# Layer 0's last output projection: channel blocks 4-7 first in its first chunk, weights in half tiles, added rows in two pools

## The chip, the cores and the metric

The kernel runs on one core of a Trainium2 chip. The metric is the device time of one execution in microseconds, given as the median of several runs. One execution was recorded by the hardware profiler; its rows are counted from the start of its span.

## The reference, cut to what matters

The reference is one inference step of a two-layer decoder trunk (a hybrid layer 0, a sparse-attention layer 1) over 1024 prompt tokens and 8 sample tokens; the kernel treats them as one row of T = 1032 columns. Layer 0 has two branches, an SSD branch that gives y_a and a convolution branch that gives y_b, and ends with one output projection over both and a layer norm of the residual sum:

```
y = y.reshape(b, l, SSD_INNER) * silu(z_a)
y = y.reshape(b, l, SSD_GROUPS, SSD_INNER // SSD_GROUPS)
y = y * rsqrt(mean(square(y), -1, keepdims=True) + EPS)
y_a = y.reshape(b, l, SSD_INNER) * norm_g
...
out = concatenate([y_a, y_b], axis=-1) @ w_out
x_new = layer_norm(ALPHA * x + out, ln_g, ln_b)
```

The mean is taken per group: SSD_GROUPS is 2, so y_a's 1024 channels are two groups of 512. All arithmetic is in float32.

## The kernel before, in words

**Layout.** Channels lie on the 128 partitions, so 1024 channels are 8 blocks of [128, 1032]. Tokens are handled in three chunks of 344 columns (CH, line 22). A matrix product in full precision is three products: each operand is split into a high part in float32r and a low part that is the rest (hi by a ScalarE cast, lo by a subtraction on VectorE or GpSimd), and `mm3` (lines 125 to 135) adds w_hi x a_hi, w_hi x a_lo and w_lo x a_hi over the 8 channel blocks kt: 24 products for one output block m of one chunk. They stand on lines 132, 133 and 134 whoever calls `mm3`.

**Weights.** `load_half` (lines 101 to 110) loads half of a weight tile (512 columns, 4 channel blocks of one output block) into the staging ring `wst` of the pool `wpool` (3 buffers), casts it (L108) to `whi` and subtracts (L109) to `wlo`, 3 buffers each. All projections go through this ring, layer 1's too.

**The end of layer 0.** The output projection is cut in two. `out_b(m)` (lines 728 to 738) multiplies y_b's 8 blocks, held as 16 tiles `act` of the pool R1, with the weights OB + m, adds ALPHA times x (L737, VectorE) and stores the rows to the DRAM tensor `dpart` (L738). This is done while the SSD heads still run. Between the calls stands `gate(g, t0, n)` (lines 701 to 718), the gated norm of one group of one chunk: it loads four blocks of silu(z_a) from DRAM (L707), multiplies (L708, VectorE), squares (L709, ScalarE), adds the squares (L711, VectorE), takes the mean over the partitions with a product by a constant matrix (L714, TensorE), takes Ln and Exp (L174 and L175, ScalarE, each with a table load), and scales the four blocks (L718, VectorE). Blocks 4 to 7 (group 1) are finished first: out_b(1) to out_b(3) are followed by gate(1, ...) of the three chunks, out_b(4) to out_b(6) by gate(0, ...).

Then `halves` (lines 754 to 767) splits y_a into tiles `ya`: blocks 4 to 7 in whole rows, blocks 0 to 3 chunk by chunk (L756 casts on ScalarE; L757 subtracts, odd blocks on GpSimd, even ones on VectorE; the tiles show as yh, yl and yb). The eight weight tiles OA + m come whole, 1024 columns or 512 KB, through a pool `wst0` with 2 buffers (L775), and are cast (L776) and subtracted (L777, odd m on GpSimd) into the 16 `act` tiles of R1, which y_b leaves free after out_b(7). They stay there for the three chunks.

For each chunk the rows of `dpart` are loaded in two transfers of four blocks (L786, pool `parts0`, 4 buffers), each output block m gets its 24 products (L790) in a PSUM tile, `pp` (2 buffers) for even m and `pt` (5 buffers) for odd m, VectorE adds it to the rows (L791), and `layer_norm` (lines 800 to 833) follows; it writes x1 as new halves into `ya` and the rows to `dx1` by a DMA of GpSimd's queue (L793). Layer 1 begins with products of x1 (L158 for its indexer keys, L938 to L940 for its values).

**What sets the order.** Each engine runs its instructions in the order of its own queue, and every DMA here but L793 is issued by SyncE (SP), also in order. The order is not that of the program text: the program is built with a planner (`TileContext(nc, schedule_with_timeline_sim=True)`, line 1766) that walks through a simulated time and, on each engine, takes what is ready, what is earlier in the text first. Tiles of a pool are handed on from user to user, and a later pool takes the place of a closed one; who takes a place waits for the last user of it. `tc.issue_after(ins)` puts the instructions of a block that are on the engine of `ins` behind `ins`.

## Time and profile before

| | us |
|---|---|
| runs: median of 3 (lowest to highest) | 1704.07 (1701.54 to 1705.91) |
| the profiled execution | 1705.27 |
| its span, by which the rows count | 1703.5 |
| mean granted clock of TensorE in it | 0.973 of full speed |

The end of the OB products and the OA products lie at about 794 to 918 us of the span. In the rows, an engine is PE (TensorE; PEld is its weight load), DVE (VectorE), ACT (ScalarE), POOL (GpSimd) or SPq (SyncE issuing DMAs); L714 is line 714 of the kernel; `out<-in` are tiles by the program's names. Products overlap in TensorE's pipeline, so a product's own length is longer than the time between two starts.

### The profile page before, as it was taken

The page shows a single profiled execution, that of the slowest core. Times are in us where ns is not written, and L with a number is a line of the kernel's source. Part 1 is how long each engine was busy: PE and PEld are TensorE (multiplying, and loading weights), DVE is VectorE, ACT ScalarE, POOL GpSimd, SP SyncE. Part 2 cuts the span into 40 slices and gives each one's busy share as a digit, 9 for nine tenths or more (in the row PEclk, how much of TensorE's full clock was granted, in tenths as well). Part 3 has the DMA queues.
Part 4 walks back from the last instruction along what each step waited for, and adds up shares of the span by engine and source line. Part 5 has one row for each costly group of instructions (what it writes and reads, how often), then busy time and mean ns, then how long its engine had stood idle before and what let it go on. Part 6 is the DMA issues. An engine that isn't in the chain of part 4 may idle for free. (4 is left out here: it accounts for less than half of the span.)

```text
span 1703.5 us, 28787 instructions
## 1 busy us (share of the span) xinstructions
PE 1598.4 (94%) x10334; PEld 1437.5 (84%) x10334; DVE 1175.5 (69%) x2480; ACT 869.4 (51%) x1950; POOL 333.9 (20%) x670
## 2 busy tenths in 40 slices
PE   8999989989999998997998999888898899999996
PEld 7999989989999987996998999878897567676774
DVE  4788987460558787756565458999957866565663
ACT  5245523552445564535334445577774755545663
POOL 4000000001122243122422200144361410112120
PEclk9999999999999999998999999999999999999998
DMA  7332243453111254433421214422346424543460
GB/s 237 105 116 66 62 112 100 133 207 117 45 38 58 70 191 157 128 114 123 151 69 54 87 46 133 128 94 88 119 148 194 113 47 114 128 109 88 99 144 28
DMA packets 165650, 185.74 MB, mean 109 GB/s; under 512 B 20324, under 2 KB 131260, under 8 KB 165252
## 3 DMA queue, kind: packets, MB, share of 16 engines
q1 hardware_dynamic: 162996, 178.15, 35.4%
q0 software_dynamic: 1216, 4.37, 0.7%
q8 instruction: 81, 1.33, 0.3%
q10 hardware_dynamic: 1296, 1.38, 0.3%
q14 instruction: 61, 0.50, 0.1%
HBM read 131.91 MB, written 54.05 MB: 109 GB/s over the span
## 5 line engine op out<-in xcount | busy, mean ns | idle before, releaser
L132 PE MATMUL pp<-act,whi 128*128 128x344 f32 x1016 | 330.2, 327 | 12.5 <-ACT act L233 8.1
L134 PE MATMUL pp<-act,wlo 128*128 128x344 f32 x1016 | 331.1, 328 | 11.0 <-DVE wlo L109 11.0
L133 PE MATMUL pp<-act,whi 128*128 128x344 f32 x1016 | 330.4, 325 | 1.0 <-POOL act L726 0.8
L132 PEld LDWEIGHTS pp<-act,whi 128*128 128x128 f32 x1016 | 194.1, 192 | 15.8 <-ACT act L233 8.1
L134 PEld LDWEIGHTS pp<-act,wlo 128*128 128x128 f32 x1016 | 194.3, 192 | 13.3 <-DVE wlo L109 11.9
L133 PEld LDWEIGHTS pp<-act,whi 128*128 128x128 f32 x1016 | 194.3, 191 | 3.5 <-POOL act L726 1.1
L108 ACT CAST whi<-wst 128x512 fp32r<-128x512 f32 x148 | 90.8, 617 | 142.4 <-PE pp L133 64.9
L334 DVE SCALAR_TENSOR_TENSOR uv<-uv,cst,uv 128x1024 f32<-128x1024 f32 x120 | 158.0, 1317 | 2.6
L132 PE MATMUL pp<-yh,whi 128*128 128x344 f32 x408 | 134.8, 330 | 7.2 <-DVE ev L1080 4.6
L109 DVE TENSOR_TENSOR wlo<-wst,whi 128x512 fp32r<-128x512 f32 x104 | 71.5, 692 | 101.2 <-ACT whi L108 101.1
L134 PE MATMUL pp<-yh,wlo 128*128 128x344 f32 x408 | 133.6, 327 | 2.2 <-DVE wlo L109 2.1
L1370 DVE CUSTOM_DVE_ANT_0 P<-lg,w 128x512 f32<-128x512 f32 (+3 forms) x144 | 82.6, 597 | 44.0 <-PE lg L1369 35.9
L1369 PE MATMUL lg<-w,Q 128*128 128x512 f32 (+3 forms) x384 | 103.7, 376 | 7.5 <-DVE nmx L1370 7.5
L132 PEld LDWEIGHTS pp<-yh,whi 128*128 128x128 f32 x408 | 78.9, 193 | 11.9 <-DVE ev L1080 6.0
L109 POOL TENSOR_TENSOR wlo<-wst,whi 128x512 fp32r<-128x512 f32 x44 | 58.2, 1324 | 156.3 <-ACT whi L108 145.4
L1405 PE MATMUL pv<-ph,V 128*64 128x256 f32 (+1 forms) x640 | 82.6, 374 | 6.0 <-DVE yo L1423 3.5
L1374 ACT ACTIVATE P<-P,mx 128x1024 f32<-128x1024 f32 (+3 forms) x64 | 63.3, 990 | 48.7 <-DVE mx L1373 47.2
L1396 PE MATMUL tr<-cst,P 128*128 128x128 f32 x576 | 85.8, 282 | 1.1 <-ACT P L1374 0.6
L1396 PEld LDWEIGHTS tr<-cst,P 128*128 128x128 f32 x576 | 65.5, 143 | 24.2 <-issue 15.3
L1369 PEld LDWEIGHTS lg<-w,Q 128*128 128x128 f32 x384 | 63.9, 194 | 25.4 <-DVE nmx L1370 13.7
L134 PEld LDWEIGHTS pp<-yh,wlo 128*128 128x128 f32 x408 | 78.9, 193 | 3.9 <-DVE wlo L109 3.1
L1197 ACT ACTIVATE jka<-S,canda 128x640 bf16<-128x640 f32 (+2 forms) x96 | 68.7, 715 | 20.8 <-POOL canda L1219 16.2
(577 smaller groups left out, 4010.4 us busy)
## 6 DMA issues: line engine op xcount, KB each, us to landing
wst<-in_W SPq DMA_DIRECT2D x148, 256.0 KB, 2.9
Q<-dq SPq DMA_DIRECT2D x64, 256.0 KB, 4.2
dq<-ev SPq DMA_DIRECT2D x48, 172.0 KB, 1.9
q<-in_ck SPq DMA_DIRECT2D x64, 128.0 KB, 2.3
vp<-in_cv SPq DMA_DIRECT2D x64, 128.0 KB, 2.1
xst<-in_xT SPq DMA_DIRECT2D x8, 516.0 KB, 9.7
dzb<-ob SPq DMA_DIRECT2D x24, 172.0 KB, 2.2
uv<-dzb SPq DMA_DIRECT2D x8, 516.0 KB, 4.2
```

Of the source, the lines that this page charges most:

```text
L108: nc.scalar.copy(hi, st)
L109: (eng or nc.vector).tensor_tensor(lo, st, hi.bitcast(F32), op=ALU.subtract)
L132: nc.tensor.matmul(out, wh, ah, start=(start and kt == 0), stop=False)
L133: nc.tensor.matmul(out, wh, al, start=False, stop=False)
L134: last = nc.tensor.matmul(out, wl, ah, start=False, stop=(stop and kt == 7))
L334: nc.vector.scalar_tensor_tensor(out, x, w[:, j : j + 1], y, op0=ALU.mult, op1=ALU.add)
L1197: nc.scalar.activation(jk, s, AF.Sign, bias=cand.bitcast(F32)[:, j : j + 1], scale=-1.0, accum_out=cnt[:, j : j + 1])
L1369: mm = nc.tensor.matmul(lg, Q[:, 4 * a + r, :], KT[g][:, s0 : s0 + m], start=(a == 0), stop=(a == 1))
L1370: nc.vector.tensor_tensor_reduce(out=P[:, s0 : s0 + m], in0=lg, in1=M[tb][:, s0 : s0 + m], scale=-0.125, scalar=BIG, op0=ALU.add, op1=ALU. ...
L1374: nc.scalar.activation(P, P, AF.Exp, bias=mx[:, r : r + 1], scale=-1.0, accum_out=rsum[:, r : r + 1])
L1396: nc.tensor.transpose(p[:, a, r * 128 : r * 128 + 128], Ps[r][:, (sb + a) * 128 : (sb + a) * 128 + 128], k.ident)
L1405: nc.tensor.matmul(pv[64 * u : 64 * u + 64, 256 * pr + c0 : 256 * pr + c1], V[:, sb + a, g * 64 : g * 64 + 64], ph[:, a, c0:c1], start=(sb ...
```

## The change

In the first chunk, the products of the OA projection begin with the channel blocks 4 to 7 of every output block m, and the blocks 0 to 3 follow: for m = 0 to 6 the second half of the products is done one after another, each in a PSUM tile that stays open; then for each of them the first half and the add; then m = 7. `mm3` gets the list of channel blocks for this. Chunks 1 and 2 are as before.

The weights come as half tiles of 512 columns through the common ring `wst` (3 buffers) in place of whole tiles through `wst0`: 18 halves, of which the second halves of m = 0 and 1 go to `whi` and `wlo` first (their subtractions on GpSimd) and are loaded once more at the end for the later chunks. The tiles in R1 are taken in the order m = 2 to 7, 0, 1. gate(0, ...) of chunks 1 and 2 is moved behind the last out_b, each after the casts of three second halves. The rows of `dpart` for chunk 0 are loaded ahead of the first halves of the weights, and the rows lie in two pools of two buffers, one for chunks 0 and 2 and one for chunk 1, which are opened after the pool of the layer norm.

```diff
--- before.py
+++ after.py
@@ -122,16 +122,16 @@
     return hi[:, o : o + m], lo[:, o : o + m]
 
 
-def mm3(k, out, w, act, t0, n, m=128, halves=2, start=True, stop=True):
+def mm3(k, out, w, act, t0, n, m=128, halves=2, kts=range(8), start=True, stop=True):
 
     nc = k.nc
-    for kt in range(8):
+    for kt in kts:
         wh, wl = wk(w, kt, m, halves)
         ah, al = act[kt]
         ah, al = ah[:, t0 : t0 + n], al[:, t0 : t0 + n]
-        nc.tensor.matmul(out, wh, ah, start=(start and kt == 0), stop=False)
+        nc.tensor.matmul(out, wh, ah, start=(start and kt == kts[0]), stop=False)
         nc.tensor.matmul(out, wh, al, start=False, stop=False)
-        last = nc.tensor.matmul(out, wl, ah, start=False, stop=(stop and kt == 7))
+        last = nc.tensor.matmul(out, wl, ah, start=False, stop=(stop and kt == kts[-1]))
     return last.ins
 
 
@@ -739,13 +739,48 @@
 
     for m in range(8):
         out_b(m)
-        if 1 <= m <= 6:
+        if 1 <= m <= 4:
             gate(1 - (m - 1) // 3, *CH[(m - 1) % 3])
+
+
+
+
+    first = [load_half(k, A["W"][OA + m], 1, eng=nc.gpsimd)[0] for m in range(2)]
+    W = {m: [None, None] for m in range(8)}
+    place = {}
+
+    def weights(h, ms):
+        for m in ms:
+            if m not in place:
+                place[m] = [k.t(R1, [128, T], F32R, "act", 16) for _ in range(2)]
+            hi, lo = (a[:, h * 512 : h * 512 + 512] for a in place[m])
+            full = k.t(k.wpool, [128, 512], F32, "wst", 3)
+            nc.sync.dma_start(full, A["W"][OA + m].rearrange("p k c -> p (k c)")[:, h * 512 : h * 512 + 512])
+            cast = nc.scalar.copy(hi, full)
+            (nc.gpsimd if m % 2 else nc.vector).tensor_tensor(lo, full, hi.bitcast(F32), op=ALU.subtract)
+            W[m][h] = hi, lo
+        return cast.ins
+
+    for ms, (t0, n) in zip((range(2, 5), range(5, 8)), CH[1:]):
+        with tc.issue_after(weights(1, ms)):
+            gate(0, t0, n)
     ssd_es.close()
     ob_es.close()
-    wst = es.enter_context(k.pool("wst0"))
-    parts = es.enter_context(k.pool("parts0"))
     op = es.enter_context(k.pool("outp0"))
+    parts = [es.enter_context(k.pool(f"parts{j}")) for j in range(2)]
+
+    dx1 = k.t(dram, [8, 128, T], F32, "dx1")
+
+    def rows(sl):
+
+        prs = [k.t(parts[sl.start == 344], [128, 4, 344], F32, "part", 2) for _ in range(2)]
+        for h, pr in enumerate(prs):
+            nc.sync.dma_start(pr, dpart[4 * h : 4 * h + 4, :, sl].rearrange("m p t -> p m t"))
+        return prs
+
+    prs = rows(slice(0, 344))
+    weights(0, range(8))
+    weights(1, range(2))
 
 
     yh_pool = k.y_es.enter_context(k.pool("yh", side="right"))
@@ -767,30 +802,29 @@
             halves(i, t0, n)
 
 
-    W = []
-    for m in range(8):
-        hi = k.t(R1, [128, T], F32R, "act", 16)
-        lo = k.t(R1, [128, T], F32R, "act", 16)
-        full = k.t(wst, [128, 1024], F32, "wst", 2)
-        nc.sync.dma_start(full, A["W"][OA + m].rearrange("p k c -> p (k c)"))
-        nc.scalar.copy(hi[:, :1024], full)
-        (nc.gpsimd if m % 2 else nc.vector).tensor_tensor(lo[:, :1024], full, hi[:, :1024].bitcast(F32), op=ALU.subtract)
-        W.append([(hi[:, :512], lo[:, :512]), (hi[:, 512:1024], lo[:, 512:1024])])
-    dx1 = k.t(dram, [8, 128, T], F32, "dx1")
     for t0, n in CH:
         sl = slice(t0, t0 + n)
-        part, prs = [], []
-        for h in range(2):
-            pr = k.t(parts, [128, 4, 344], F32, "part", 4)
-            prs.append(pr)
-            nc.sync.dma_start(pr, dpart[4 * h : 4 * h + 4, :, sl].rearrange("m p t -> p m t"))
-            part += [pr[:, m, :] for m in range(4)]
-        for m in range(8):
-            p = pt(k)[:, :n] if m % 2 else pp(k)
-            mm3(k, p, W[m], ya, t0, n)
-            nc.vector.tensor_tensor(part[m], part[m], p, op=ALU.add)
+        if t0:
+            prs = rows(sl)
+        part = [prs[m // 4][:, m % 4, :] for m in range(8)]
+        if t0 == 0:
+            ps = []
+            for m in range(8):
+                p = pt(k)[:, :n] if m in (1, 3, 4, 5, 6) else pp(k)
+                mm3(k, p, [None, first[m]] if m < 2 else W[m], ya, t0, n, kts=(4, 5, 6, 7), stop=False)
+                ps.append(p)
+                if m < 6:
+                    continue
+                for j in range(7) if m == 6 else (7,):
+                    mm3(k, ps[j], W[j], ya, t0, n, kts=(0, 1, 2, 3), start=False)
+                    nc.vector.tensor_tensor(part[j], part[j], ps[j], op=ALU.add)
+        else:
+            for m in range(8):
+                p = pt(k)[:, :n] if m % 2 else pp(k)
+                mm3(k, p, W[m], ya, t0, n)
+                nc.vector.tensor_tensor(part[m], part[m], p, op=ALU.add)
         layer_norm(k, op, part, n, t0 + n == T, lambda m: [a[:, sl] for a in ya[m]],
-                   lambda h: nc.gpsimd.dma_start(dx1[4 * h : 4 * h + 4, :, sl].rearrange("m p t -> p m t"), prs[h]))
+                   lambda h, prs=prs, sl=sl: nc.gpsimd.dma_start(dx1[4 * h : 4 * h + 4, :, sl].rearrange("m p t -> p m t"), prs[h]))
     es.close()
     r1_es.close()
     k.x1 = ya
```

## Rows read from the trace of the kernel before

**Rows 1.** The page, part 1: busy time, share of the span, instructions of each engine.

```profile
PE 1598.4 (94%) x10334; PEld 1437.5 (84%) x10334; DVE 1175.5 (69%) x2480; ACT 869.4 (51%) x1950; POOL 333.9 (20%) x670
```

**Rows 2.** Windows of 3 us, 794 to 845: busy time (instructions), clock, DMA, GB/s.

```profile
803.00:806.00 3.00, 0.81 (x2) 0.00 (x0) 0.17 (x1) 2.13 (x3) 0.00 (x0) 0.50 1.04 401
...
sum 51.00, PE 37.89 PEld 34.98 DVE 36.12 ACT 22.56 POOL 25.83; mean PE 2.23 PEld 2.06 DVE 2.12 ACT 1.33 POOL 1.52
```

**Rows 3.** TensorE's timeline: start, length, instruction, count [idle before it <- releaser].

```profile
795.97 0.32 PE L134 MATMUL pp<-act,wlo 128*128 128x344 f32 x1
802.29 1.52 PE L714 MATMUL pm<-gz,o 128*128 128x344 f32 x2 [6.00 <-DVE gz L711]
807.18 0.66 PE L132 MATMUL pp<-yh,act 128*128 128x344 f32 x1 [3.38 <-ACT act L776]
...
809.45 0.65 PE L134 MATMUL pp<-yh,act 128*128 128x344 f32 x1 [1.33 <-DVE act L777]
...
813.34 0.38 PE L132 MATMUL pp<-yh,act 128*128 128x344 f32 x1
...
815.85 0.42 PE L134 MATMUL pt<-yh,act 128*128 128x344 f32 x1 [0.55 <-POOL act L777]
...
817.20 0.74 PE L714 MATMUL pm<-gz,o 128*128 128x344 f32 x2
...
830.02 0.43 PE L134 MATMUL pt<-yh,act 128*128 128x344 f32 x1 [1.85 <-POOL act L777]
...
834.13 0.32 PE L133 MATMUL pp<-yb,act 128*128 128x344 f32 x1
...
848.32 0.32 PE L134 MATMUL pt<-yh,act 128*128 128x344 f32 x1
```

**Rows 4.** VectorE's timeline, same columns.

```profile
795.09 4.16 DVE L757 TENSOR_TENSOR yl<-yb,yh 128x1032 fp32r<-128x1032 f32 x2
799.17 0.50 DVE L737 SCALAR_TENSOR_TENSOR ob<-ob,pp 128x344 f32<-128x344 f32 x1
...
801.73 0.50 DVE L711 TENSOR_TENSOR gz<-gz,gz 128x344 f32<-128x344 f32 x1
```

**Rows 5.** ScalarE's timeline, same columns.

```profile
795.06 0.49 ACT L709 ACTIVATE gz<-ya 128x344 f32<-128x344 f32 x1
...
803.84 0.55 ACT L174 ACTIVATE gz<-pm,epsb 128x344 f32<-128x344 f32 x1 [5.70 <-PE pm L714]
...
806.10 1.03 ACT L776 CAST act<-wst 128x1024 fp32r<-128x1024 f32 x1
...
838.77 1.05 ACT L776 CAST act<-wst 128x1024 fp32r<-128x1024 f32 x1 [8.23 <-DMA wst<-in_W]
```

**Rows 6.** SyncE's timeline: DMA issues.

```profile
800.07 0.93 SPq L775 DMA_DIRECT2D wst<-in_W  x2
```

**Rows 7.** Tiles yl and yh: shortest/median/longest ns, first and last start.

```profile
L757 DVE TENSOR_TENSOR yl<-yb,yh x2: 1219/2116/3014, 795.1 to 798.0; 128x1032 fp32r<-128x1032 f32 x2
...
L757 POOL TENSOR_TENSOR yb<-ya,yh x6: 911/1198/5211, 799.4 to 831.1; 128x344 fp32r<-128x344 f32 x6
```

**Rows 8.** The page, parts 5 and 6, then DMA issues of 780 to 850 us.

```profile
L108 ACT CAST whi<-wst 128x512 fp32r<-128x512 f32 x148 | 90.8, 617 | 142.4 <-PE pp L133 64.9
...
L109 DVE TENSOR_TENSOR wlo<-wst,whi 128x512 fp32r<-128x512 f32 x104 | 71.5, 692 | 101.2 <-ACT whi L108 101.1
...
L109 POOL TENSOR_TENSOR wlo<-wst,whi 128x512 fp32r<-128x512 f32 x44 | 58.2, 1324 | 156.3 <-ACT whi L108 145.4
...
wst<-in_W SPq DMA_DIRECT2D x148, 256.0 KB, 2.9
...
wst<-in_W SPq DMA_DIRECT2D x8, 512.0 KB, 4.6
part<-dpart SPq DMA_DIRECT2D x4, 688.0 KB, 7.5
```

**Rows 9.** TensorE's timeline, the start of chunk 2.

```profile
888.10 0.43 PE L132 MATMUL pp<-yh,act 128*128 128x344 f32 x1 [0.67 <-DVE part L791]
```

## The prediction

> **What bounds the kernel now.** The page's first part says TensorE: 94% busy [rows 1]. The reader should see that work moved beside it gains nothing; only time in which TensorE stands, or runs at a lower clock, can be won. The change touches one seam: the end of the OB products (out_b) and the first chunk of the OA products. I cut that seam, 794 to 845 us, into 3 us windows: TensorE is busy 37.9 of 51 us, and from 803 to 806 its granted clock is 0.50 of full speed, 1.2 GHz instead of 2.4 [rows 2].
>
> TensorE's own timeline says where the 13.1 us went [rows 3]. The last OB product starts at 795.97. Then it stands 6.00 before the gate's sum of squares (L714), 3.38 before the first OA product (released by the weight cast L776), then 1.33, 0.55 and 1.85 before products that want the low part of a weight (L777). At the end of the chunk, from 834.13 to 848.32, 90 products start, 0.158 apart. From 809.45 to 813.34 there are 13 starts, 0.30 apart: 3.9 us instead of 2.1, 1.8 lost to the clock. From 830.02 to 834.13 there are 15: 4.1 instead of 2.4, 1.7 lost. The first L714 took 1.52 where the second took 0.74, and the two products from 807.18 lost some 0.5 more. Clock in all: 4.8. **The seam loses 17.9 us**, the most that any cure of it can give.
>
> Why the first 9.4 of it: the gate of chunk 1 shares every queue with the weights. VectorE did two whole-row subtractions (4.16 us) and an evacuation first, so that gate's last sum came at 801.73 [rows 4]. ScalarE stood 5.70 at its Ln, and only then came the first weight cast, at 806.10 [rows 5]. SyncE issued the first OA weights at 800.07, right behind a store that needed the evacuation of 799.17 [rows 4, 6]. Three queues hold the weights back, while blocks 4 to 7 of the activations are complete by 799.2: VectorE's two subtractions start at 795.1 and 798.0, the longer is 3.01 [rows 7].
>
> **The change part by part, against the profiled execution.** It took 1705.27 us (span 1703.5), 1.2 above the median of 1704.07.
>
> 1. Start with blocks 4-7. The first 84 products of the chunk (12 for each of m=0 to 6) need no gate of group 0, and the weights of m=0 and 1 go through the common staging ring: their loads can be issued while out_b(7) runs, and wait for nothing of the pools that close there. TensorE can start when block 4's low part is there, 795.1+3.0 = 798.1 [rows 7]: it stands 1.8 instead of 9.4. The old stand of 1.85 was followed by 1.7 at the low clock [rows 3], so I add that. Block 6 ends at 799.2, when only four slow products are through: nothing more. New loss 3.5. The old one was 9.4 and 3.1 of clock (0.8, 0.5, 1.8), 12.5. **Gain 9.0.**
>
> 2. Half tiles. One lands in 2.9 us (median of 148), its cast takes 0.62, its subtraction 0.69 on VectorE or 1.32 on GpSimd [rows 8]: about 5 us for a slot, and three slots give a half every 1.7 us. TensorE uses one in 12 x 0.158 = 1.9. The ring just keeps up, so of the old 1.33+0.55+1.85 and 1.7 of clock (5.4) some must stay. Best: 0. Worst: the last old cast waited 8.23 for its load [rows 5], queued with the rows (two transfers of 688 KB, 7.5 us each [rows 8]); such a wait once, with 1.7 of clock, is 9.9. I take 2.7, half the old, since the same rows are still in the queue but three halves stand ahead. **Gain 2.7.**
> The count of instructions: 18 halves instead of 8 wholes. ScalarE 18 x 0.62 against 8 x 1.04 [rows 5, 8], 2.8 us more; GpSimd subtracts ten halves, 13.2 us in all; VectorE eight, 5.5. In the 51 us ScalarE was busy 22.6 and GpSimd 25.8, the latter with four wholes of its own among them [rows 2]. So these hide; without that cover it is 3 us for each engine. Ten more loads cost SyncE 3 us of issuing, beside its waits.
> On size, the rows give 2.9 us for 256 KB and 4.6 for 512 KB [rows 8]. The Trainium skill, "DMA: Bandwidth & Descriptors", section Bandwidth, asks for transfers of 1 MiB or more and so speaks against halving; the rows agree that the bytes per microsecond fall (88 KB against 111), and by the rule alone the gain of this point would go.
>
> 3. Gates of chunks 1 and 2. Their ScalarE work is put behind casts (of m=4, then of m=7). Behind it wait VectorE's scaling, the halves of blocks 0 to 3 in these chunks, and no product until chunk 1, some 30 us after the start. But L714 lies in TensorE's queue: if the squares are late, first-chunk products behind it stand, and ScalarE's casts behind the Ln with them. Below: 0, as at the second L714, which waited for nothing. Above: 6.00 each, as at the first. I take 2.0 in all, nearer the one without wait, since 84 products stand ready around them. **Loss 2.0.**
>
> 4. Rows in two pools, loaded early. Their adds begin when m=0 has both halves, about 798.1+1.7+96 x 0.158 = 815; no product needs a freed PSUM tile until m=7, some 12 us later, which covers a late landing. Chunk 2's rows still wait for chunk 0's store. TensorE's wait of 0.67 there [rows 9] should go, as chunk 0 now ends before chunk 1 starts. **Gain 0.7**, bounds 0 and 0.7.
>
> 5. PSUM and places. Seven tiles are open at once (five pt, two pp); the heads, which use pt too, end before. The weights lie in R1 in the order 2 to 7, 0, 1, so layer 1's first tiles, laid over them, are released up to two m (48 products, 7.6 us) later within chunk 2. They are cast while the last norm runs, which I take as the cover: 0; at worst 7.6.
>
> Sum: 9.0+2.7-2.0+0.7 = 10.4. **1705.3-10.4 = 1694.9 for an execution like the profiled one; 1.2 less, 1693.7, for the median.** All of layer 1 hangs on this output, so the shift should reach the end.
>
> **Rivals.** A. The weights set the pace. Before, eight casts ran from 806.10 to 838.77 [rows 5]: 32.7 us for 14 halves, 2.33 each. At that pace 16 halves last 37.3 from 798.1, to 835.4. Chunk 0 ended at 848.5 with 12 products of chunk 1 among its own, so at 846.4 without. That gains 11.0, less 2.0 for the gates and two more falls of the clock (3.4): 5.6, **1698.5**. For it: GpSimd's subtraction of the same piece took from 0.91 to 5.21 us [rows 7]. Against: part of the old pace was the queue, not the engines. The Trainium skill, "SBUF — State Buffer", section "SBUF: two separate sides", says that GpSimd and a VectorE instruction with two SBUF inputs lock each other out for a whole instruction, which would bring this case about; the spread of that row agrees.
>
> B. The start does not move. If SyncE still issues the halves only behind the last out_b store (800.07), the first is ready at 800.1+2.9+0.6+1.3 = 804.9, 2.3 before the old start, and the rest is as before: **1701.8**. Against: the ring is common, and three slots can be filled before.
>
> C. The gates hold TensorE. From the fourth square (795.06) to the weight cast (806.10) [rows 5] was 11.0 us. If TensorE stands for that whole chain at one gate and 6.0 at the other, with 1.7 of clock each, it is 20.4; with 3.5 and 2.7 the seam loses 26.6 instead of 17.9: 8.7 slower, **1712.8**. It decides from a total of some 12 us at the two L714; beyond that the gain is gone. For it: casts, squares and sums lie in full queues. Against: only one gate was late before, behind two subtractions.
>
> **How the numbers follow.** A measurement of this kernel tells some 0.3% (5.1 us) from no change: faster is below 1699.0. Forecast 0.60, A 0.18, B 0.10, C 0.12. The forecast is faster nearly always (0.57), A half the time (0.09), B seldom (0.01): 0.67. C is slower, 0.12; the rest, 0.21, the same. Range: the low end is the whole seam won, 17.9+0.7 off 1704.1 = 1685.5, unlikely to the last microsecond, so 1686; the high end takes in A and B and, with 6 us lost at each gate, the forecast's bound short of C (1693.7+10.0 and the clock's 1.7): 1706.
>
> **What would show it.** Right: TensorE stands at most 3 us before the first OA product, whose weight is one of the common ring (whi, wlo); loads of halves issued before 795; the low clock over by 805; chunk 0's products through near 836. Wrong: L714 with a wait over 5 us (C); the first OA product after 804 (B); many waits of 1 to 2 us on GpSimd's weight subtraction, with the clock between 0.5 and 0.8 (A). A gain in the seam that is missing at the end would mean that layer 1 was held by something else.

## The result, and the profile after

The changed kernel takes **1694.16 us** (median of 4 runs, 1691.48 to 1695.80) where the kernel before takes 1702.80 on the same chip (4 runs, 1701.52 to 1705.91): a ratio of **0.9945, 95% interval 0.9924 to 0.9965**. The prediction said 1693.7. The number was right, but by luck: the gain lies elsewhere than the prediction said, and the rest of this document is about that.

The profiled execution of the changed kernel took 1691.48 us, its span is 1689.3, TensorE's mean granted clock 0.979 (before: 0.973). The page's first part shows the same engine in the same share:

```profile
PE 1592.6 (94%) x10334; PEld 1433.3 (85%) x10334; DVE 1170.9 (69%) x2484; ACT 871.2 (52%) x1960; POOL 335.7 (20%) x676
```

To find where the time went I cut both traces at the same five products of TensorE: the last head product (L625), the first product of the mean of chunk 0, of chunk 1 and of chunk 2 (`sum` times the constant matrix in `layer_norm`), and layer 1's first score product. That gives four stretches, called here the **seam**, **chunk 1**, **chunk 2** and the **last norm**. Windows of the kernel before over these four (length, then busy time and count of each engine; the third number from the end is the clock):

```profile
790.30:848.48 58.18, 45.07 (x247) 41.98 (x246) 39.45 (x51) 25.90 (x38) 28.03 (x76) 0.85 0.47 158
848.48:882.97 34.49, 34.49 (x216) 33.89 (x215) 23.30 (x46) 11.40 (x20) 8.94 (x10) 1.00 0.08 22
882.97:916.46 33.49, 32.64 (x201) 31.47 (x200) 23.63 (x47) 12.60 (x22) 10.23 (x13) 1.00 0.27 95
916.46:975.20 58.74, 53.06 (x354) 49.55 (x353) 24.54 (x55) 24.87 (x52) 11.18 (x15) 0.94 0.27 85
```

The same windows of the changed kernel:

```profile
789.20:847.23 58.03, 45.06 (x256) 42.10 (x254) 38.03 (x55) 28.50 (x50) 29.38 (x17) 0.94 0.47 146
847.23:880.85 33.62, 33.62 (x199) 32.45 (x199) 23.51 (x47) 12.03 (x21) 8.65 (x10) 0.96 0.19 66
880.85:912.98 32.13, 32.13 (x200) 31.37 (x199) 23.52 (x46) 12.17 (x21) 10.64 (x15) 1.00 0.30 94
912.98:966.70 53.72, 52.04 (x364) 48.97 (x363) 25.61 (x57) 24.90 (x53) 9.59 (x77) 1.00 0.28 88
```

The four together are 184.9 us before and 177.5 after: 7.4 less. The seam, which the change rewrites, is as long as before (58.2 and 58.0); it holds nine more products, at 0.158 us each [rows 3], so at equal products it is 1.6 us shorter. Chunk 1 has 17 products fewer and is only 0.9 shorter, at equal products 1.8 longer: the two together gain nothing. **5.0 of the 7.4 lie in the last norm**, which has ten more products, and for which the change writes no order.

Outside the four, the two spans differ by 6.7 us more, half of it in a stretch of layer 1's attention (from the first product into a tile `lg` to the first product of its output projection) that no edit here touches. The windows over it of the kernel before, of the changed kernel and of experiment 2 below:

```profile
1301.28:1375.75 74.47, 61.71 (x371) 40.55 (x368) 65.27 (x154) 48.73 (x76) 23.27 (x14) 0.93 0.53 145
1292.18:1363.06 70.88, 60.70 (x371) 39.74 (x368) 62.05 (x154) 49.01 (x77) 23.12 (x14) 0.95 0.55 156
1290.22:1363.55 73.33, 63.27 (x372) 41.34 (x368) 62.24 (x154) 49.11 (x77) 23.11 (x14) 0.91 0.53 150
```

Twelve of the 14 kernels profiled, the last two of these rows among them, run this stretch in one and the same order on all four engines; it took 70.9, 71.7 or 73.5 us with a granted clock of 0.95, 0.93 or 0.91, so this part is the clock of the execution. The kernel before and experiment 4 run it in other orders and took 74.5 and 76.0 at 0.93: the planner placed work anew here too, which is some 2.8 us of the profiled difference at a like clock, from one execution of each. The medians are the measure of the total.

**The seam.** TensorE's timeline of the changed kernel, its waits [rows 3 for before]:

```profile
795.34 0.31 PE L132 MATMUL pp<-yh,whi 128*128 128x344 f32 x1
797.09 0.43 PE L133 MATMUL pp<-yl,whi 128*128 128x344 f32 x1 [1.44 <-DVE yl L792]
...
802.49 0.66 PE L134 MATMUL pp<-yh,act 128*128 128x344 f32 x1 [2.87 <-DVE act L760]
...
816.12 0.43 PE L132 MATMUL pp<-yh,act 128*128 128x344 f32 x1 [0.30 <-ACT act L759]
...
818.43 0.42 PE L134 MATMUL pp<-yh,act 128*128 128x344 f32 x1 [1.73 <-DVE act L760]
...
824.32 0.43 PE L134 MATMUL pt<-yh,act 128*128 128x344 f32 x1 [2.27 <-POOL act L760]
...
847.23 1.52 PE L841 MATMUL pt<-sum,o 128*128 128x344 f32 x2 [4.30 <-DVE sum L839]
```

The first product starts with no wait, its weight from the common ring. The old waits of 6.00 and 3.38 are gone. But six others sum to 12.91 us, where the old ones summed to 13.11. VectorE's timeline shows two of the causes:

```profile
794.01 4.17 DVE L792 TENSOR_TENSOR yl<-yb,yh 128x1032 fp32r<-128x1032 f32 x2
798.10 0.50 DVE L737 SCALAR_TENSOR_TENSOR ob<-ob,pp 128x344 f32<-128x344 f32 x1
798.52 2.60 DVE L792 TENSOR_TENSOR yb<-ya,yh 128x344 fp32r<-128x344 f32 x2
801.04 1.39 DVE L760 TENSOR_TENSOR act<-wst,act 128x512 fp32r<-128x512 f32 x1
...
837.40 3.08 DVE L718 SCALAR_TENSOR_TENSOR ya<-ya,cst,gz 128x344 f32<-128x344 f32 x4 [4.03 <-ACT gz L175]
```

The low part of the third weight (801.04) stands behind two halves of chunk 0 (798.52, 2.60 us) that no product wants yet: TensorE's 2.87. And the last adds and sums of chunk 0 stand behind the scaling of the moved gate of chunk 2, which waited 4.03 for its Exp: TensorE's 4.30. That Exp is late because of ScalarE's queue. The product that its Ln needs, the second L714, ran at 828.83, but the Ln stands behind weight casts that waited 7.37 and then 2.09 for their loads:

```profile
829.05 1.94 ACT L759 CAST act<-wst 128x512 fp32r<-128x512 f32 x3 [7.37 <-DMA wst<-in_W]
...
833.72 1.28 ACT L174 ACT_TABLE_LOAD   x1
```

GpSimd's timeline shows a third cause:

```profile
816.52 6.52 POOL L792 TENSOR_TENSOR yb<-ya,yh 128x344 fp32r<-128x344 f32 x2 [4.28 <-ACT yh L791]
823.01 2.51 POOL L760 TENSOR_TENSOR act<-wst,act 128x512 fp32r<-128x512 f32 x2
```

Two halves of chunk 1, not due for 30 us, take 6.52 (5.38 the first of them alone, 1.18 the second) ahead of a weight's low part that TensorE waits for (2.27). The low part behind them frees a staging buffer at 824.27, and SyncE asks for the next half at 824.29: this is the load for which ScalarE waited 7.37. So the third cause stands behind part of the 4.30 as well.

**The last norm.** In the kernel before TensorE stood 5.67 us for the first square of chunk 2, and then ran at 0.50 of its clock, 1.2 GHz, until about 929. This is ScalarE's timeline of the kernel before there:

```profile
921.63 0.85 ACT L927 CAST w<-eq 128x792 fp32r<-128x792 f32 x1 [3.20 <-DMA eq<-in_wv]
922.38 0.47 ACT L912 CAST ki<-ev 64x344 fp32r<-64x344 f32 x1
922.88 0.48 ACT L913 CAST ki<-ev 64x344 fp32r<-64x344 f32 x1
923.38 1.25 ACT L814 ACTIVATE sq<-part 128x344 f32<-128x344 f32 x3
```

and TensorE's:

```profile
923.93 1.52 PE L816 MATMUL pt<-sq,o 128*128 128x344 f32 x2 [5.67 <-ACT sq L814]
```

The squares stand behind a cast of layer 1's value weights, which waits for its load, and behind casts of ki, layer 1's indexer keys. In the changed kernel ki's copies and casts come later (from 937) and only the weight cast stands ahead. ScalarE:

```profile
916.73 0.85 ACT L961 CAST w<-eq 128x792 fp32r<-128x792 f32 x1 [14.05 <-DMA eq<-in_wv]
917.49 1.25 ACT L848 ACTIVATE sq<-part 128x344 f32<-128x344 f32 x3
```

and TensorE, which now has ki products behind the mean (19 of 48 stand ahead of it, before it was 29):

```profile
918.03 0.84 PE L850 MATMUL pt<-sq,o 128*128 128x344 f32 x2 [1.68 <-ACT sq L848]
```

The wait is 4.0 us shorter, and no half clock follows. The second part of that is not the order's doing. Experiments 2, 3 and 4 below run the last norm in the same order as the changed kernel on all four engines, with waits of 1.81 to 1.83, and there the clock fell and the stretch took 55.4 us where it is 53.7 here; experiment 2:

```profile
914.01 0.84 PE L853 MATMUL pt<-sq,o 128*128 128x344 f32 x2 [1.81 <-ACT sq L851]
```

So of the 5.0 us some 1.7 hang on whether the clock falls in the one execution. The change writes no order for ki; the planner placed it anew, presumably because the work ahead of it had moved. My theory for the experiments: **the gain is this accident of order in the last norm; the seam itself gave about a microsecond, since what the early start won was given back to other queue orders.** The rival is the prediction: the start with blocks 4-7 and the half tiles pay for themselves.

### The profile page after: what moved, and what is told of

Read it like the earlier page. It is cut to its first block, busy times and chain, and to the rows that moved or that the text cites. A ratio compares the mean times of both kernels' runs of the same rounds, so it can differ in the third digit from the quotient of the medians.

```text
span 1689.3 us, 28852 instructions
## 1 busy us (share of the span) xinstructions
PE 1592.6 (94%) x10334; PEld 1433.3 (85%) x10334; DVE 1170.9 (69%) x2484; ACT 871.2 (52%) x1960; POOL 335.7 (20%) x676
## 5 line engine op out<-in xcount | busy, mean ns | idle before, releaser
L132 PE MATMUL pp<-act,whi 128*128 128x344 f32 x1016 | 329.8, 326 | 12.5 <-ACT act L233 8.1
```

Of the source, the lines that this page charges most:

```text
L132: nc.tensor.matmul(out, wh, ah, start=(start and kt == kts[0]), stop=False)
```

## The experiments

All medians below stand beside runs of the kernel before on the same chip (1703.44 for the first four, 1703.79 for the next, 1703.57 for the last four; 17 to 19 runs each; the experiments have 5 to 12, and the changed kernel its own four beside 1702.80). Lengths in us from the profiled execution, products of TensorE in the seam in brackets.

| kernel | median | ratio, 95% | seam | chunk 1, 2 | last norm |
|---|---|---|---|---|---|
| before | 1703.6 | | 58.2 (247) | 34.5, 33.5 | 58.7 |
| changed | 1694.16 | 0.9945 (0.9924-0.9965) | 58.0 (256) | 33.6, 32.1 | 53.7 |
| 1 before, ki late | 1692.38 | 0.9938 (0.9909-0.9966) | 58.1 (247) | 34.5, 30.5 | 54.8 |
| 2 low part first | 1691.80 | 0.9933 (0.9906-0.9960) | 55.3 (256) | 32.3, 32.2 | 55.4 |
| 3 blocks in order | 1700.62 | 0.9987 (0.9972-1.0003) | 62.2 (240) | 34.4, 32.1 | 55.4 |
| 4 two staging rings | 1694.00 | 0.9947 (0.9932-0.9962) | 56.9 (251) | 32.9, 32.1 | 55.4 |
| 5 gates early | 1691.60 | 0.9919 (0.9902-0.9936) | 53.6 (243) | 33.9, 32.3 | 57.9 |
| 6 one pool, ahead | 1698.32 | 0.9969 (0.9954-0.9984) | 63.0 (259) | 31.5, 32.1 | 56.3 |
| 7 = 2 + GpSimd | 1689.23 | 0.9917 (0.9900-0.9935) | 54.0 (255) | 33.8, 32.1 | 53.8 |
| 8 = 7 + ki late | 1691.58 | 0.9926 (0.9910-0.9942) | 55.9 (255) | 33.7, 30.7 | 55.3 |
| 9 before, blocks 4-7 | 1696.99 | 0.9965 (0.9950-0.9980) | 58.0 (246) | 33.2, 32.3 | 54.5 |
| 10 = 7 + gates early | 1688.99 | 0.9918 (0.9898-0.9938) | 49.9 (238) | 35.1, 32.2 | 53.7 |
| 11 = 10 + ki late | 1688.37 | 0.9907 (0.9887-0.9927) | 50.2 (239) | 35.1, 30.7 | 55.3 |
| 12 one pool, behind | 1698.30 | 0.9974 (0.9963-0.9984) | 63.0 (259) | 31.5, 32.2 | 57.9 |

Only the interval of experiment 3 lies clear of the changed kernel's, so the medians alone order few of these kernels. The stretches carry more, though each is one execution: where two kernels have the same order in the last norm and the clock does the same, the length agrees within 0.1 us (53.7 in the changed kernel, 7 and 10; 55.4 in 2, 3 and 4).

**1. The kernel before, with ki's products behind the last norm's mean.** Nothing else changed:

```
+    k.mean = <second mean product of layer_norm>.ins
+    with tc.issue_after(k.mean):
         ki(*CH[0])
         ki(*CH[1])
```

> The kernel before, with one thing changed: the key products of layer 1 (ki, chunks 0 and 1) stand on TensorE behind the mean of layer 0's last norm. Tail theory: the change gained most of its time here and not at the seam (last norm's sum to first score product: 58.9 us before, 53.9 after), because these products now fill TensorE while ScalarE squares, and ScalarE is free of their copies. Then this kernel gets about 4 to 5 us faster than before (1698), the stretch falls to 54 to 55 us and TensorE's wait of 5.67 before the squares' products is gone or under 2. Seam theory (my prediction): the tail plays no part; 1702.8 within 2 us, and the wait only moves.

It took 1692.38, less than expected and as little as the changed kernel, with not one line of the change in it. The seam and chunk 1 are as before; chunk 2 and the last norm are 6.9 us shorter together, and the stretch in layer 1's attention runs in the changed kernel's order here as well. ScalarE's timeline of this kernel:

```profile
913.76 1.33 ACT L814 ACTIVATE sq<-part 128x344 f32<-128x344 f32 x3 [10.62 <-DVE part L812]
...
916.34 0.86 ACT L927 CAST w<-eq 128x792 fp32r<-128x792 f32 x1
```

The squares now stand ahead of the weight cast, and ki's casts come after it. Over the last norm TensorE is busy to the end, at full clock:

```profile
911.78:966.60 54.82, 54.82 (x381) 52.04 (x382) 26.60 (x56) 25.30 (x53) 12.28 (x17) 1.00 0.29 96
```

So an order of this kind, with what the planner makes of it further on, is worth what the whole change is worth. The reverse, the changed kernel with ki in the order of before, was not run. Which of the two casts ahead of the squares costs more wasn't tried by itself; in the kernel before, the ki casts are 1.0 us of the 5.67 and the load of the value weights is the larger part.

**2. The changed kernel, with the low part of the third weight ahead of the halves on VectorE** (`lows[h, m]` is the subtraction of half h of weight m).

```
+    with tc.issue_after(lows[1, 2]):
         halves(i, t0, n)
```

> The changed kernel, with VectorE's and GpSimd's order forced in one place: the chunk-wise halves of blocks 0 to 3 stand on VectorE behind the low part of weight m=2. Queue theory: the changed kernel's wait of 2.87 us at 802.5 and its low clock are VectorE's order alone; the wait falls below 0.5, the fourth half is issued near 799 instead of 802.5, and the seam gets 3 to 5 us shorter; total 1689 to 1691. Rival (the seam's end is set elsewhere): the wait goes, but the 4.30 us before the first norm's sum grows by as much; total 1693 to 1695.

TensorE's wait fell from 2.87 to 0.24, the seam by 2.8 us; the total is 2.4 lower, which the runs can't tell from none. The wait at the mean did not grow, as the rival had it, but fell from 4.30 to 1.54, with the gates still moved. Other waits took part of this back: two on weight casts (1.90 and 1.24), and the one behind GpSimd's halves (two of them take 6.51 us again), 2.27 in the changed kernel, here in TensorE's timeline:

```profile
823.24 0.65 PE L134 MATMUL pt<-yh,act 128*128 128x344 f32 x1 [3.39 <-POOL act L761]
```

**3. The changed kernel, with chunk 0 in the order of before** (24 products for one m after the other; half tiles, moved gates and two pools kept).

```
-        if t0 == 0: <blocks 4-7 of all m, then blocks 0-3>
+        for m in range(8): mm3(all eight blocks)
```

> The changed kernel with part 1 undone: chunk 0 takes all eight blocks of an m together, as before; half tiles, gates and row pools stay. Seam theory: the order of blocks is worth the 9.0 us of my sum, so this is at 1702 to 1704 and TensorE stands some 10 us before the first OA product again. Tail theory: the seam has hardly gained, its end is set by the weights and VectorE; this is within 3 us of the changed kernel (1691 to 1697), with the waits at other places.

1700.62: nearly all of the gain is gone. TensorE's timeline:

```profile
810.05 1.51 PE L714 MATMUL pm<-gz,o 128*128 128x344 f32 x2 [13.19 <-DVE gz L711]
...
817.08 0.65 PE L132 MATMUL pp<-yh,act 128*128 128x344 f32 x1 [5.52 <-ACT act L759]
```

With the gates behind the last `out_b` and no order to fill the time, TensorE stands 13.19 us at the gate: this is rival C of the prediction, and the order of the blocks is what keeps it away. Part of the loss is the loads' order, which this kernel keeps: the second halves still come first, and the 5.52 is a wait for the first half of a weight. So this prices the order inside the change, not the order by itself (experiment 9 does). The last norm stays short (55.4), so the two gains are separate.

**4. The changed kernel, with the first halves through a staging ring of their own** (three buffers beside the common three).

> The changed kernel with the first halves of the weights (and the two reloaded) in a staging pool of their own of three tiles, so six slots in place of three. If the ring of three sets the pace after the first halves (ScalarE waited 9.88, 7.37 and 2.09 us for loads), casts come earlier, the last gate's Ln follows earlier than 835, the wait of 4.30 before the first norm's sum shrinks to under 1.5, and the total is 1688 to 1691. If GpSimd's and VectorE's subtractions set it, the loads come earlier but the low parts do not: 1693 to 1696.

1694.00, no difference. The wait of 2.87 is still there, so it was VectorE's order and not the ring. The casts ahead of the last gate's Ln waited less for their loads (2.51 and 4.74), the Ln came 4.3 us earlier (830.73), and the 4.30 at the mean went, as expected of the ring. But SyncE now asks for the rows of chunk 0 at 826.03 and 835.22 in place of 799.00 and 802.96, so the first adds stand behind the gate's scaling (833.12 to 835.16), and this came instead:

```profile
836.49 0.66 PE L132 MATMUL pp<-yh,act 128*128 128x344 f32 x1 [6.99 <-DVE part L821]
```

**5. The changed kernel, with the gates of chunks 1 and 2 back in the loop of `out_b`.**

```
-        if 1 <= m <= 4:
+        if 1 <= m <= 6:
...
-    for ms, (t0, n) in zip((range(2, 5), range(5, 8)), CH[1:]):
-        with tc.issue_after(weights(1, ms)):
-            gate(0, t0, n)
+    weights(1, range(2, 8))
```

> The changed kernel with the gates of chunks 1 and 2 of blocks 0-3 back in the loop of output projection B, where they stood before; all the rest as changed. The prediction's part 3 priced the move of the gates at a loss of 2.0 us, so by it this kernel takes 1692, 2 us less than the changed one. The theory from the two traces: the gates' vector work was off the path before (it ran under projection B's products) and the move makes room for early loads and casts only; the wait for the mean of the norm of chunk 0 (4.30 us in the changed kernel, VectorE's adds behind a gate) goes to about 1.5 us, and the seam (head products to the mean of chunk 0, 58.0 us) becomes 55 to 56. The rival: with the gates early the casts of the half tiles lie behind the gates' squares on ScalarE, the first product of projection A waits 2 us or more where it waited for nothing, and the seam is 59 to 61 us, the total 1695 to 1697. The stretch from the mean of chunk 2 to the first score product stays 53 to 55 us by both.

1691.60: by the medians the move costs 2.6 us, but the two intervals overlap. In the seam it costs more, 4.5 (53.5 against 58.0; with 13 products fewer, 2.4), and the wait at the mean of chunk 0 is gone altogether. The last norm lost again, for ScalarE's old reason (the weight cast ahead of the squares waits for its load until 914.58), and the clock fell:

```profile
915.87 1.52 PE L848 MATMUL pt<-sq,o 128*128 128x344 f32 x2 [3.40 <-ACT sq L846]
```

**6 and 12. The changed kernel, with the rows in one pool of four,** opened ahead of the norm's pool as before (6), or behind it (12).

```
-    parts = [es.enter_context(k.pool(f"parts{j}")) for j in range(2)]
+    parts = es.enter_context(k.pool("parts0"))
```

> The changed kernel with the rows to add in one pool of four buffers, opened ahead of the norm's pool, as before; all the rest as changed. The prediction's part 4 priced the two pools and the early rows at a gain of 0.7 us. By that this kernel takes 1695, 0.7 us more, which is less than the runs can tell; in the trace the rows of chunks 0 and 1 are loaded as early as in the changed kernel, and the stages of chunks 0, 1 and 2 stay within 1 us of 58.0, 33.6 and 32.4 us. The rival: two pools matter for which release the first loads wait for; with one pool the rows of chunk 0 come late, the adds of chunk 0 wait for a transfer, and the seam is 60 us or more, the total 1697 or more.

> The changed kernel with the rows to add in one pool of four buffers that is opened behind the norm's pool, where the two pools are opened. With one pool ahead of it the rows of chunk 0 were asked for at 837.74 us of the span where the changed kernel asks at 799.00 and 802.96, TensorE waited 7.38 us for the adds, and the seam was 63.0 us. If the place counts (ahead of the norm's pool the rows lie where the moved gates still hold their tiles), one pool behind it asks for them near 800 again, the seam is 57 to 59 us, and the total 1693 to 1696. The rival: the number of pools counts (one pool's second pair or its first holds the other up), the rows come at 837 again and the total is 1697 to 1699.

Both took 1698.3, 4.1 more, with the same seam of 63.0: the number of pools counts, not the place. Against the changed kernel the seam is 5.0 longer and chunk 1 2.1 shorter; the last norm is longer too, by 2.6 and 4.2. SyncE's timeline of the first shows the rows of chunks 0 and 1 asked for together, those of chunk 0 36 to 39 us late:

```profile
813.66 17.73 SPq L758 DMA_DIRECT2D wst<-in_W  x8
...
837.74 2.78 SPq L778 DMA_DIRECT2D part<-dpart  x4
```

where the changed kernel asks for the first at 799.00:

```profile
799.00 0.43 SPq L778 DMA_DIRECT2D part<-dpart  x1
802.46 0.33 SPq L758 DMA_DIRECT2D wst<-in_W  x1
802.96 0.37 SPq L778 DMA_DIRECT2D part<-dpart  x1
```

TensorE then needs the PSUM tiles that the adds have not freed, and the clock falls as well:

```profile
843.34 0.65 PE L132 MATMUL pp<-yh,act 128*128 128x344 f32 x1 [7.38 <-DVE part L820]
```

Why one pool puts the load behind all those weights in SyncE's queue the trace doesn't settle (it names a store of `dx1`, far off). That the tiles of the moved gates still hold part of the one pool's place is likely, since in the changed kernel the rows of chunk 1 wait for the gate's L718; it is only argued.

**7. Experiment 2, and GpSimd's halves of chunks 1 and 2 behind its last weight.**

```
-            with tc.issue_after(lows[1, 2]):
+            with tc.issue_after(lows[1, 1 if i % 2 and t0 else 2]):
```

> The kernel of the second experiment (on VectorE, the low part of the third weight tile ahead of the chunk-wise halves) and, on top, GpSimd's halves of blocks 1 and 3 for chunks 1 and 2 behind its last weight subtraction. In the second experiment GpSimd took 6.51 us for two such pieces from 815.46 and TensorE then waited 3.39 us for the weight subtraction behind them. If that queue order is the cause, the wait of 3.39 goes, TensorE stays at full clock over that place, and the seam is 51 to 53 us where it was 55.3; the total 1688 to 1690. The rival: what slows GpSimd is VectorE's work at the same time, so the weight subtractions themselves take longer and TensorE waits for them, 2 us or more, at other products, the seam staying at 54 to 56; or the adds of chunk 1 wait for the late halves and the stage of chunk 1 grows from 32.3 to 35 or more.

The wait of 3.39 is gone, the seam is 54.0, the total 1689.23. But the clock did not stay up (0.50 from 815.75 to 822.57), the wait at the mean is 3.11 where experiment 2 had 1.54, and chunk 1 is 1.5 us longer: seam and chunk 1 together are as in experiment 2, and the last norm, in the same order, is 1.6 shorter because the clock did not fall there. The slow piece of GpSimd is not gone; it is now a pair of weights, 5.61 us (4.08 and 1.57) where the pair before it took 2.98:

```profile
808.14 2.98 POOL L761 TENSOR_TENSOR act<-wst,act 128x512 fp32r<-128x512 f32 x2 [4.54 <-ACT act L760]
816.88 5.61 POOL L761 TENSOR_TENSOR act<-wst,act 128x512 fp32r<-128x512 f32 x2 [5.76 <-ACT act L760]
```

So both sides of the expectation were partly right: the order in the queue made the wait, and what slows GpSimd belongs to the time, not to the instruction. In that time VectorE works without a break, from 815.11 to 819.8, on additions, products and subtractions of two tiles in SBUF; GpSimd's long piece ends at 820.96, after that break. The Trainium skill, "SBUF — State Buffer", section "SBUF: two separate sides", says that such an instruction and one of GpSimd lock each other out; these rows agree on GpSimd's side (5.61 against 2.98). VectorE's pieces were not held up in that time (0.51 each); that it is locked out too does not show in them.

**8. Experiment 7, with ki late as in experiment 1.**

> The kernel before this one, and on TensorE the products of ki of chunks 0 and 1 behind the mean of the last norm, as in the first experiment. If the changed kernel and its variants already fill the last norm (53 to 55 us from the mean of chunk 2 to the first score product, TensorE at full clock), nothing is left there: that stretch stays 53 to 55 us, and the total is that of the kernel before within 2 us. The rival: 19 of 48 products that still stand ahead of the norm cost their own time, 19 x 0.16 = 3 us, and the total falls by 2 to 3 us to 1686.

1691.58, last norm 55.3 with 19 products more, chunk 2 as much shorter (30.7): the two together are 86.0 us where they were 85.9, so nothing is left to win there. The total is 2.4 higher, a little over the 2 that were allowed; 1.9 of the profile's difference lie in the seam, ahead of the edit. Where the last norm is already filled, the edit of experiment 1 brings nothing, which is what the theory says.

**9. The kernel before, with the order of the blocks alone** (whole tiles, gates, rows and pools as before).

```
-        for m in range(8): mm3(all eight blocks)
+        if t0 == 0: <blocks 4-7 of all m, then blocks 0-3>
```

> The kernel before with one part of the change alone: chunk 0 of projection A takes blocks 4-7 of all eight outputs first, then blocks 0-3; whole weight tiles, gates, rows and pools as before. The prediction's part 1 gave 9.0 us of the 10.4 to this start. By the trace of before the first product of A waited 3.38 us more for the cast of the first whole weight tile after the gate's mean had come (6.00 us), so without the early half tiles the order has nothing to start on: the seam (58.2 us from the head products to the mean of chunk 0) falls by 1 us or less, or grows, since one half of chunk 0's products now wants all eight weights in half the time, and the total is 1702 to 1706. The rival, by the prediction's part 1 as worded: the order is what counts, the seam falls to 52 or below and the total to 1695.

The seam did what the theory said: 58.0, with the very waits of before. TensorE's timeline:

```profile
802.33 1.52 PE L714 MATMUL pm<-gz,o 128*128 128x344 f32 x2 [6.00 <-DVE gz L711]
807.22 0.65 PE L132 MATMUL pp<-yh,act 128*128 128x344 f32 x1 [3.38 <-ACT act L776]
```

Nothing is there to start on, since the weights are not cast. Yet the total is 1696.99, 6.6 less, and I had said 1702 to 1706: the planner placed ki anew here too. The first square waits 2.81, the clock stays up, and the last norm is 54.5 instead of 58.7 (chunks 1 and 2 are 1.2 us shorter each, and the attention of layer 1 runs in the changed kernel's order):

```profile
919.76 0.84 PE L828 MATMUL pt<-sq,o 128*128 128x344 f32 x2 [2.81 <-ACT sq L826]
```

An edit in the seam that gains nothing there gains behind it, most of it in the last norm: the clearest sign of what carried the result.

**10 and 11. Experiment 7 with the gates early (10), and with ki late on top (11).**

> The kernel with both queue orders mended (low part of the third tile first on VectorE, GpSimd's late halves behind its weights; 1689.2 us, seam 54.0) with the gates of blocks 0-3 back in the loop of projection B, as in the kernel with the gates alone moved back (seam 53.5, total 1691.6). If the two gains are separate, the waits of 2.73 and 1.82 us of the latter go too, the seam is 50 to 52 us and the total 1686 to 1688. The rival: both mend the same wait (the adds of chunk 0 late on VectorE), the sum takes no more than either, seam 53 to 54 and total 1689 to 1691.

> The kernel before this one with ki of chunks 0 and 1 behind the mean of the last norm on TensorE. With the gates moved back alone, the stretch from the mean of chunk 2 to the first score product was 57.6 us, with a wait of 3.40 us for the first square and TensorE at half clock after it; where 29 of 48 products of ki stood behind the mean it was 53 to 55. So if the kernel before this one has 57 us there, this one has 54 to 55 and its total is 2 to 3 us less; if it has 53 to 54 there, nothing is gained. The rival: the wait for the square is ScalarE's own (its copies ahead of the square), and the stretch stays 57.

The seam of the first is the shortest of all, 49.9, at clock 0.97:

```profile
788.80:838.69 49.89, 41.88 (x238) 38.52 (x236) 39.78 (x52) 27.19 (x47) 23.44 (x15) 0.97 0.50 166
```

It holds 18 products fewer than the changed kernel's, so it is worth 5.3 us less; their totals are 1688.99 and 1688.37, 14.6 and 15.2 below the kernel before. Against experiment 7 they gain no more than the runs can tell (part of the shorter seam is in chunk 1, 35.1). With ki late on top nothing is gained, as expected where the last norm is 53.7: chunk 2 and the last norm together are 86.0 us where they were 85.8. Against the changed kernel the ratio of the second is 0.4% lower, and the intervals just touch. It is the fastest median here.

## Why the prediction was right, and where it was wrong

The sum was 10.4 us, the medians fell by 8.6. Four of its five steps were off, and a gain that it did not have made up for them. That the number came out is luck.

**Step 1, the early start: gain 9.0 said, 6.6 found.** The start moved as said: no wait at the first product, then 1.44 for block 4's low part where the step had 1.8. The step failed at "nothing more": it followed blocks 4 to 7 and the weights of m=0 and 1, and not the weight of m=2, whose low part stood behind VectorE's halves for 2.87 us. That wait brought the half clock, 11 products from 802.49 to 805.78, 1.5 us more than at 0.158 each. New loss 5.9 against 3.5 said; the old one was 12.5.

**Step 2, half tiles: gain 2.7 said, none found.** The waits on weights are 0.30, 1.73 and 2.27, with about 1.1 of half clock near 820: 5.4, exactly what whole tiles lost. Its picture was a ring of three that just keeps up by the mean times of its instructions. What counted was when a buffer came free, and that was set by the order within VectorE's and GpSimd's queues (experiment 2 won 2.8 in the seam; the 1.3 that experiment 7 won there it lost again in chunk 1). More buffers did not shorten the total (experiment 4), but that kernel also asks for the rows late, so it does not clear the ring. The prediction had read that GpSimd's subtraction of the same piece takes from 0.91 to 5.21 [rows 7], but kept it for rival A. The Trainium skill ("DMA: Bandwidth & Descriptors", section Bandwidth) asks for transfers of 1 MiB or more, which speaks against this gain. The gain did go, but for another reason, so these runs don't show the rule.

**Step 3, the moved gates: loss 2.0 said, 2.6 by the medians of experiment 5**, whose intervals overlap; 2.4 in the seam at equal products. The size was near, the place wrong. No L714 waited in the changed kernel. What waited was the mean of chunk 0, 4.30, because VectorE's adds stood behind the gate's scaling. The step named that scaling and said that no product needs it until chunk 1; what it left out is what is queued behind it on the same engine, and that the Ln ahead of it queues behind casts that wait for loads. The gates alone don't make the 4.30: with the same gates it is 1.54 in experiment 2.

**Step 4, the rows: 0.7 said, 4.1 measured** (experiments 6 and 12; 2.9 of it in the seam and chunk 1, the last norm being longer too). The wait of 0.67 at chunk 2 [rows 9] is gone as said. But the step priced only the early landing, as if the rows would come in time with one pool. With the moved gates they would not, and its bound above was too low.

**Step 5, places: 0.** "They are cast while the last norm runs, which I take as the cover": the last norm was taken for a place that hides work. It was the place with the largest avoidable wait after the seam, 5.67 us and the half clock. The first view should have been the waits of the whole tail of layer 0, not of 794 to 845 alone; the row of 923.93 was there to be read.

Steps 1 to 3 as found give 6.6 + 0 - 5.8 (the 4.30 and about 1.5 of half clock behind it, which falls into chunk 1) = 0.8 for the seam and chunk 1; the windows of the two say 1.0, and nothing at equal products. The last norm gave 5.0, and 6.6 at equal products, of which some 1.7 is the clock that did not fall. Chunk 2 gave 1.4, and the attention of layer 1 some 2.8 by its other order. Together this is more than the 8.6 of the medians; one profile of each kernel does not divide it closer.

**Rivals.** A (the weights set the pace) was true in part: one wait of 2.27 on GpSimd's subtraction, not many. B did not happen: the first halves were asked for at 779.59 and 781.58. C did not happen, and experiment 3 shows its wait (13.19) as soon as the order of the blocks is taken away, though not its price (1700.62 against 1712.8). Of the signs named, the first three held (the low clock was over at 805.73) and chunk 0's products, said to be through near 836, ended near 839.5; the low clock came back twice, at 820 and 847.

## What to carry to other kernels

Where a planner orders the queues, an edit moves work far from where it stands: cut both traces at the same landmarks through to the end before you credit the edit, and put the suspected order alone into the old kernel (experiment 1), which is what told the causes apart here. Then compare the order of instructions of the stretches that no edit touches: here equal orders with unequal times went with another clock, and unequal orders showed the planner's hand. Before pricing an early start, ask of every engine what stands ahead of the second and third thing it needs, not only the first. And a step whose cost is hidden "under" another stage needs that stage's own waits read first.

## What the runs showed of the hardware that I had not expected

- The length of a wait alone did not say whether TensorE's clock falls. In the last norm it stayed at full after 1.68 (changed), 1.74 (experiment 7), 1.65 (10) and 2.81 (9); it fell to 0.50, 1.2 GHz, at 1.81 and 1.83 (2, 3 and 4) and at 3.31 to 5.67 (5, 6, 12, before). The stretch was 53.7 to 54.5 us in the first group and 55.4 to 58.7 in the second. The changed kernel, 7 and 10 have the very order of 2, 3 and 4 there, and waits within 0.2 us of theirs: 53.7 against 55.4.
- A pair of GpSimd subtractions that takes 2.98 us took 5.61 while VectorE worked without a break on SBUF tiles, and two smaller ones 6.52; in both pairs the first alone was long (4.08 and 5.38). VectorE's own pieces were not longer in experiment 7.
- In a stretch of layer 1 that no edit touches, twelve kernels with the same order on all four engines took 70.9 to 73.5 us, at a granted clock of 0.95 down to 0.91. One profile against another is no measure of so small a gain unless order and clock are compared as well.
